# HGRN2 output products of a hybrid decoder layer: the eight products within the chunk first, then the eight with the state, all adding into one PSUM bank

## The chip, the cores and the metric

One core of one Trainium2 chip runs the whole program. The time is the device time of one execution in microseconds (us); less is better. TensorE (PE) multiplies, VectorE (DVE), ScalarE (ACT) and GpSimd (POOL) do the rest, SyncE (SP) issues the transfers.

## The reference, cut to what matters

One decoder layer: RMSNorm, a projection whose columns feed four mixers (S5, HGRN2, RWKV-7, pooling), an output projection, and a squared-ReLU MLP. There are 2048 prompt tokens, 32 sample tokens, width 1024, and four HGRN2 heads of 64. The change touches the HGRN2 mixer alone, which the reference computes chunk by chunk:

```python
o = jnp.einsum('bhts,bhsv->bhtv', att, vb) + jnp.einsum('bhtk,bhkv->bhtv', qb * jnp.exp(b), S)
b_last = b[:, :, -1:, :]
S = jnp.exp(b_last[:, :, 0, :])[..., None] * S + jnp.einsum('bhsk,bhsv->bhkv', kb * jnp.exp(b_last - b), vb)
```

The output `o` of a chunk is a sum of two products: the attention within the chunk with the values, and the scaled queries with the state `S` that the chunk before left. The state then moves on.

## The kernel before, in words

Tokens run in six blocks of 256 or 384 (the last also carries the 32 sample tokens). Each block goes through projection, mixers, output projection and MLP; the mixers of block b+1 are woven between the MLP products of block b. The large products (helper `mmg`, lines 157 to 159) take a split of both operands into a high and a low part, so that each weight tile gives three products of 128 rows by 128 columns of the array. Their weights arrive by DMA (`raw`), ScalarE makes the high part (`whi`, line 128), VectorE the low part (`wlo`, line 129). A scheduler at build time puts the recorded instructions of all lanes into one order for each engine, and each engine then works in that order, waiting on semaphores where it has to.

HGRN2 goes by pairs of chunks of 64 tokens (`hgrn_pair`): 2048 / 128 = 16 pairs, each with 4 heads h, of which head h lies in column j = h // 2 and on partitions 0 to 63 or 64 to 127 (hp = h % 2). At the end of a pair stand three sets of eight small fp32 products, which this text calls by their lines in the kernel before:

- line 1294, `pu`: what the pair adds to the state, `VK` (128 rows, 64 columns) with `VB`. Line 1297 on VectorE makes of it the state after chunk 0 and after chunk 1 of the pair (`S[1]` and `S[2]`; `S[0]` is left over from the pair before).
- line 1303, **inner products** in what follows: `VB` with the attention in `v`, into `po`. Each takes all 128 rows of the array and 64 of its columns, starting at column 0 for even heads and at column 64 for odd ones.
- line 1304, **state products**: `S[cp]` with the scaled queries `Q0`, added to the same place in `po`. Each takes 64 rows and 64 columns. With cp = 0 they need `S[0]`, with cp = 1 they need `S[1]`.

An fp32 product is two records in the trace, so eight products are 16 records, and the 16 pairs make 256 records of each line. `po` lies in one PSUM bank; `hgrn_out` then has ScalarE copy it (line 1407).

Of the kernel before, what the change touches and what calls it, by code (L numbers as in the profile page):

```python
# [606 lines left out]
class Mix(Main):  # L607
# [580 lines left out]
    def hgrn_pair(self, b, c0, pool):  # L1188
        nc = self.nc
        tt, ts, stt = nc.vector.tensor_tensor, nc.vector.tensor_scalar, nc.vector.scalar_tensor_tensor  # L1190
        act, mm = nc.scalar.activation, nc.tensor.matmul
# [5 lines left out]
        q, f, v, gt = P[:, 2:4, W], P[:, 4:6, W], P[:, 6:8, W], P[:, 8:10, W]  # L1197
# [17 lines left out]
        Q0 = T("lf")  # L1215
# [14 lines left out]
        VK, VB = T("VK", (128, 4, 64)), self.VB  # L1230
# [22 lines left out]
        for l0, l1 in ((-1, 2), (2, 6)):  # L1253
            pas = [self.px() for _ in range(2)]
            sec = {}
            for l in range(l0, l1):
                o0 = 0 if l < 0 else 64 * (l - l0) + (64 if l0 < 0 else 0)
                w = 64 if l < 0 else 32
                for hp in range(2):
# [3 lines left out]
                    for j in range(2):  # L1263
                        for cp in range(2):
                            o = 128 * j + 64 * cp
                            if l < 0:
                                a, c = k[hs, j, 64 * cp:64 * cp + 64], q[hs, j, 64 * cp:64 * cp + 64]
                            else:
                                h = LV[l]
# [6 lines left out]
            for l in range(l0, l1):  # L1276
                for hp in range(2):
                    o, d = v[:, :, 64 * hp:64 * hp + 64], sec[l, hp]
# [3 lines left out]
                    h = LV[l]  # L1282
# [6 lines left out]
        S = [self.S[:, (self.Si + i) % 3] for i in range(3)]  # L1289
        self.Si = (self.Si + 2) % 3  # L1290
        pu = self.px()[:, :256].rearrange("p (c j n) -> p c j n", c=2, j=2)
        for h in range(4):
            for cp in range(2):
                mm(pu[64 * (h % 2):64 * (h % 2) + 64, cp, h // 2, :], VK[:, h, :], VB[:, cp, h, :], start=True, stop=True)
        for cp in range(2):
            for j in range(2):
                stt(out=S[cp + 1][:, j, :], in0=S[cp][:, j, :], scalar=eb[:, j, 64 * cp + 63:64 * cp + 64], in1=pu[:, cp, j, :], op0=ALU.mult, op1=ALU.add)
        po = self.px()[:, :256].rearrange("p (j n) -> p j n", j=2)
        for h in range(4):
            o, j = slice(64 * (h % 2), 64 * (h % 2) + 64), h // 2  # L1300
            for cp in range(2):
                w = slice(64 * cp, 64 * cp + 64)
                mm(po[o, j, w], VB[:, cp, h, :], v[:, j, o], start=True, stop=False)  # L1303
                mm(po[o, j, w], S[cp][o, j, :], Q0[o, j, w], start=False, stop=True)  # L1304
        yield
        yield from self.hgrn_out(b, W, po, 256, T)

# [728 lines left out]
```

## Time and profile before

| | |
|---|---|
| median of three runs | 2759.57 us (2753.03 to 2764.25) |
| the profiled execution | 2760.78 us, span 2758.7 us |
| PE busy | 2676.0 us, 97% of the span |
| DVE, ACT, POOL busy | 71%, 52%, 13% |
| granted TensorE clock, mean | 0.982 |

The profile comes from one execution. Busy time of PE overlaps from product to product, since the end of a product in flight is modelled; how much room a product takes is better read from the distance between the starts of neighbours in the timeline.

### The profile page before, as it was taken

The page shows a single profiled execution, that of the slowest core. Times are in us where ns is not written, and L with a number is a line of the kernel's source. Part 1 is how long each engine was busy: PE and PEld are TensorE (multiplying, and loading weights), DVE is VectorE, ACT ScalarE, POOL GpSimd, SP SyncE. Part 2 cuts the span into 40 slices and gives each one's busy share as a digit, 9 for nine tenths or more (in the row PEclk, how much of TensorE's full clock was granted, in tenths as well). Part 3 has the DMA queues.
Part 4 walks back from the last instruction along what each step waited for, and adds up shares of the span by engine and source line. Part 5 has one row for each costly group of instructions (what it writes and reads, how often), then busy time and mean ns, then how long its engine had stood idle before and what let it go on. Part 6 is the DMA issues. An engine that isn't in the chain of part 4 may idle for free.

```text
span 2758.7 us, 52873 instructions
## 1 busy us (share of the span) xinstructions
PE 2676.0 (97%) x20466; PEld 2524.8 (92%) x20466; DVE 1960.4 (71%) x4324; ACT 1438.7 (52%) x2377; POOL 359.0 (13%) x864
## 2 busy tenths in 40 slices
PE   8799899999999999999999999999999999999998
PEld 8688799999999999999999999999999989989997
DVE  6885877875877777487777648776766776666666
ACT  6554756554655445365554536554454744445443
POOL 7631201101011100101110010111001101000000
PEclk9899999999999999999999999999999999999999
DMA  6543343464322355532225553223565223535443
GB/s 204 145 127 90 121 140 130 139 212 155 117 84 90 97 170 162 163 117 86 94 94 171 163 160 110 90 90 100 168 179 163 95 93 106 147 112 174 162 168 124
DMA packets 221068, 366.27 MB, mean 133 GB/s; under 512 B 105521, under 2 KB 140913, under 8 KB 220817
## 3 DMA queue, kind: packets, MB, share of 16 engines
q1 hardware_dynamic: 220816, 362.90, 42.1%
q8 instruction: 161, 2.64, 0.4%
q14 instruction: 91, 0.74, 0.1%
HBM read 343.26 MB, written 17.99 MB: 131 GB/s over the span
## 4 chain that ended last, share of the span: by engine, by line
PE 75%; DVE 8%; DMA 5%; ACT 3%; POOL 3%; issue 3%; SPq 2%; DVEq 0%; ACTq 0%; POOLq 0%
PE mm L157 21%; PE mm L158 21%; PE mm L159 20%; DMA raw<-w 2%; DVE wlo L129 2%; PE x L1272 1%; PE x L1304 1%; ACT whi L128 1%; PE x L1303 1%; POOL tm L885 1%; POOL XD L887 1%; PE x L687 1%; DMA xs<-xT 1%; DMA mt<-dB 1%; PE x L951 1%
## 5 line engine op out<-in xcount | busy, mean ns | idle before, releaser
L128 ACT CAST whi<-raw 128x1024 fp32r<-128x1024 f32 x552 | 577.5, 1046 | 785.5 <-PE mm L158 566.2
L157 PE MATMUL mm<-AB,whi 128*128 128x384 f32 (+2 forms) x2880 | 951.6, 331 | 14.5 <-ACT whi L128 6.1
L159 PE MATMUL mm<-AB,wlo 128*128 128x384 f32 (+2 forms) x2880 | 937.4, 326 | 5.9 <-DVE wlo L129 5.9
L158 PE MATMUL mm<-AB,whi 128*128 128x384 f32 (+2 forms) x2880 | 936.3, 326 | 0.8 <-DVE AB L199 0.6
L129 DVE TENSOR_TENSOR wlo<-raw,whi 128x1024 fp32r<-128x1024 f32 x552 | 678.8, 1230 | 269.6 <-ACT whi L128 267.0
L157 PEld LDWEIGHTS mm<-AB,whi 128*128 128x128 f32 x2880 | 547.9, 191 | 27.8 <-ACT whi L128 6.8
L159 PEld LDWEIGHTS mm<-AB,wlo 128*128 128x128 f32 x2880 | 548.7, 191 | 10.7 <-DVE wlo L129 8.0
L158 PEld LDWEIGHTS mm<-AB,whi 128*128 128x128 f32 x2880 | 548.9, 191 | 6.8 <-DVE AB L199 0.9
L157 PE MATMUL mm<-act,whi 128*128 128x384 f32 (+2 forms) x1536 | 497.0, 329 | 3.3 <-DVE h L338 2.1
L158 PE MATMUL mm<-act,whi 128*128 128x384 f32 (+2 forms) x1536 | 495.8, 324 | 0.5 <-DVE act L329 0.3
L159 PE MATMUL mm<-act,wlo 128*128 128x384 f32 (+2 forms) x1536 | 493.6, 323 | 0.0
L157 PEld LDWEIGHTS mm<-act,whi 128*128 128x128 f32 x1536 | 289.3, 190 | 10.9 <-DVE h L338 2.6
L158 PEld LDWEIGHTS mm<-act,whi 128*128 128x128 f32 x1536 | 291.4, 190 | 5.5 <-issue 1.8
L159 PEld LDWEIGHTS mm<-act,wlo 128*128 128x128 f32 x1536 | 291.1, 190 | 3.9 <-issue 2.4
L338 DVE TENSOR_TENSOR h<-h,mm 128x384 f32<-128x384 f32 (+2 forms) x384 | 192.9, 510 | 114.1 <-PE mm L159 113.3
L885 POOL TENSOR_TENSOR tm<-sq,XD 32x15 f32<-32x15 f32 (+7 forms) x240 | 97.9, 408 | 571.8 <-DMA sq<-XC 554.4
L329 DVE TENSOR_TENSOR act<-q,act 128x384 fp32r<-128x384 f32 (+2 forms) x192 | 99.6, 520 | 7.4 <-ACT q L326 3.3
L324 ACT ACTIVATE act<-r 128x384 fp32r<-128x384 f32 (+2 forms) x192 | 94.1, 490 | 14.2 <-DVE r L323 12.2
L880 POOL MEMSET XD<- 32x512 f32 x16 | 8.3, 516 | 604.6 <-PE x L969 570.1
L887 POOL TENSOR_TENSOR XD<-XD,tm 32x15 f32<-32x15 f32 (+7 forms) x240 | 80.2, 334 | 18.5
L192 DVE TENSOR_TENSOR acc<-acc,sq 128x384 f32<-128x384 f32 (+2 forms) x126 | 65.0, 516 | 12.7 <-ACT sq L191 10.0
L328 DVE TENSOR_TENSOR q<-r 128x384 f32<-128x384 f32 x128 | 71.9, 562 | 1.2 <-ACT r L321 1.0
(585 smaller groups left out, 3195.1 us busy)
## 6 DMA issues: line engine op xcount, KB each, us to landing
raw<-w SPq DMA_DIRECT2D x552, 512.0 KB
xs<-xT SPq DMA_DIRECT2D x96, 192.0 KB
yT<-xo SPq DMA_DIRECT2D x32, 192.0 KB
mt<-dB SPq DMA_DIRECT2D x20, 256.0 KB
mt<-dT SPq DMA_DIRECT2D x20, 256.0 KB
mt<-dC SPq DMA_DIRECT2D x20, 256.0 KB
xs<-xT SPq DMA_DIRECT2D x24, 144.0 KB
rt<-dRot SPq DMA_DIRECT2D x16, 98.0 KB
```

What stands on the lines that cost most here:

```text
L128: nc.scalar.copy(hi, raw)
L129: (nc.gpsimd if GW(i) else nc.vector).tensor_tensor(out=lo, in0=raw, in1=hi, op=ALU.subtract)
L157: nc.tensor.matmul(ps[:, :n], a, xh, start=k == ks[0], stop=False)
L158: nc.tensor.matmul(ps[:, :n], a, xl, start=False, stop=False)
L159: nc.tensor.matmul(ps[:, :n], c, xh, start=False, stop=k == ks[-1])
L192: nc.vector.tensor_tensor(out=acc[:, :n], in0=acc[:, :n], in1=q[:, :n], op=ALU.add)
L324: nc.scalar.activation(out=self.act[:, s, 0, :n], in_=r[:, :n], func=AF.Square)
L328: nc.vector.tensor_tensor(out=q[:, :n], in0=r[:, :n], in1=r[:, :n], op=ALU.mult)
L329: nc.vector.tensor_tensor(out=self.act[:, s, 1, :n], in0=q[:, :n], in1=self.act[:, s, 0, :n], op=ALU.subtract)
L338: nc.vector.tensor_tensor(out=self.h[:, d, :n], in0=self.h[:, d, :n], in1=ps[:, :n], op=ALU.add)
L885: g.tensor_tensor(out=w, in0=U[:, 0:t, t:t + 1].to_broadcast([32, t, m]), in1=XT[:, t:t + 1, t:16].to_broadcast([32, t, m]), op=ALU.mult)
L887: g.tensor_tensor(out=XT[:, 0:t, t:16], in0=XT[:, 0:t, t:16], in1=w, op=ALU.add)
```

## The change

The eight inner products of a pair are issued one after the other, then the eight state products. Both go through the same list of (j, cp, hp), in which hp changes fastest, and line 1294 goes through it too. Since all sixteen outputs now lie open in one bank at once, only the first product on each half of the partitions starts the bank afresh (`start`), and all others add or, where nothing was written since, overwrite. The number and sizes of products stay as they were.

```diff
+        jch = [(j, cp, hp, slice(64 * hp, 64 * hp + 64)) for j in range(2) for cp in range(2) for hp in range(2)]
-        for h in range(4):
-            for cp in range(2):
-                mm(pu[64 * (h % 2):64 * (h % 2) + 64, cp, h // 2, :], VK[:, h, :], VB[:, cp, h, :], start=True, stop=True)
+        for j, cp, hp, o in jch:
+            mm(pu[o, cp, j, :], VK[:, 2 * j + hp, :], VB[:, cp, 2 * j + hp, :], start=True, stop=True)
...
-        for h in range(4):
-            o, j = slice(64 * (h % 2), 64 * (h % 2) + 64), h // 2
-            for cp in range(2):
-                w = slice(64 * cp, 64 * cp + 64)
-                mm(po[o, j, w], VB[:, cp, h, :], v[:, j, o], start=True, stop=False)
-                mm(po[o, j, w], S[cp][o, j, :], Q0[o, j, w], start=False, stop=True)
+        for j, cp, hp, o in jch:
+            w = slice(64 * cp, 64 * cp + 64)
+            mm(po[o, j, w], VB[:, cp, 2 * j + hp, :], v[:, j, o], start=j == cp == 0, stop=False, skip_group_check=True)
+        for j, cp, hp, o in jch:
+            w = slice(64 * cp, 64 * cp + 64)
+            mm(po[o, j, w], S[cp][o, j, :], Q0[o, j, w], start=False, stop=j == cp == 1, skip_group_check=True)
```

In the new kernel the inner products are line 1302 and the state products line 1305; the scheduler orders the rest anew. On PE, a pair's small products stand in two clusters with large products between them. This is the first cluster of the seventh pair (the second pair of the third block; `AB` and `whi` belong to a large product), before:

```order
L159 MATMUL mm<-AB_78,wlo 128x384
L1294 MATMUL x<-VB,VK 64x64 x8
L1303 MATMUL x<-P_7462,VB 64x64
L1304 MATMUL x<-lf,S 64x64
L1303 MATMUL x<-P_7462,VB 64x64
L157 MATMUL mm<-AB_78,whi 128x384
```

and now:

```order
L159 MATMUL mm<-AB_78,wlo 128x384
L1294 MATMUL x<-VB,VK 64x64 x8
L1302 MATMUL x<-P_7462,VB 64x64 x8
L1305 MATMUL x<-lf,S 64x64 x2
L157 MATMUL mm<-AB_78,whi 128x384
```

The six inner products that were left over for later now stand here, and the two state products on `S[0]` of column 0 follow them. The second cluster of the same pair, before, with 21 large products between the two (the alternation goes on where the dots stand, to 13 products in all):

```order
L159 MATMUL mm<-AB_78,wlo 128x384
L1304 MATMUL x<-lf,S 64x64
L1303 MATMUL x<-P_7462,VB 64x64
L1304 MATMUL x<-lf,S 64x64
...
L157 MATMUL mm<-AB_78,whi 128x384
```

and now, with 18 large products between:

```order
L159 MATMUL mm<-AB_78,wlo 128x384
L1305 MATMUL x<-lf,S 64x64 x6
L157 MATMUL mm<-AB_78,whi 128x384
L158 MATMUL mm<-AB_78,whi 128x384
L159 MATMUL mm<-AB_78,wlo 128x384
```

The six state products that are left stand alone. Fourteen of the 16 pairs have no other product inside the run of eight inner products; in the fourth and the fifth pair the scheduler now puts some. This is the fourth pair (line 800 is a product of the RWKV-7 mixer with 64 rows), before:

```order
L1294 MATMUL x<-VB,VK 64x64 x8
L1303 MATMUL x<-P_1555,VB 64x64
L1304 MATMUL x<-lf,S 64x64
L1303 MATMUL x<-P_1555,VB 64x64
L800 MATMUL x<-P_2418,wl 128x128 x2
L157 MATMUL mm<-act,whi 128x256
```

and now:

```order
L1294 MATMUL x<-VB,VK 64x64 x8
L1302 MATMUL x<-P_1555,VB 64x64 x3
L800 MATMUL x<-P_2418,wl 128x128 x2
L1302 MATMUL x<-P_1555,VB 64x64 x5
L1305 MATMUL x<-lf,S 64x64 x2
L157 MATMUL mm<-act,whi 128x256
```

The second cluster of this pair follows after 8 large products, where it followed after 17.

## Rows read from the trace of the kernel before

**Rows 1.** The page's head, engines' busy time, and chain that ended last:

```profile
span 2758.7 us, 52873 instructions
PE 2676.0 (97%) x20466; PEld 2524.8 (92%) x20466; DVE 1960.4 (71%) x4324; ACT 1438.7 (52%) x2377; POOL 359.0 (13%) x864
PE 75%; DVE 8%; DMA 5%; ACT 3%; POOL 3%; issue 3%; SPq 2%; DVEq 0%; ACTq 0%; POOLq 0%
```

**Rows 2.** Busy time by stretch: length, each engine, PE clock, DMA share, GB/s:

```profile
150.00:640.00 490.00, 466.96 (x4285) 431.70 (x4285) 377.11 (x931) 280.06 (x483) 76.69 (x181) 0.97 0.44 137
640.00:1120.00 480.00, 478.08 (x3461) 452.69 (x3460) 339.00 (x735) 251.11 (x403) 48.01 (x115) 1.00 0.40 126
2080.00:2400.00 320.00, 312.66 (x2445) 294.33 (x2444) 220.28 (x540) 162.32 (x294) 34.60 (x77) 0.97 0.41 121
```

**Rows 3.** Groups from 640 to 2400 us: records | busy us, mean ns | idle before:

```profile
L1303 PE MATMUL x<-P,VB 128*64 128x64 f32 x176 | 28.6, 245 | 0.0
```

**Rows 4.** Chain that ended last, by line, from 640 to 2400 and from 150 to 640:

```profile
by line: PE mm L157 25.7%; PE mm L158 24.8%; PE mm L159 24.7%; PE x L1272 1.7%; PE x L1304 1.3%; PE x L1303 1.2%; PE x L687 1.1%; DMA raw<-w 1.0%; issue 0.9%; PE x L1827 0.7%; PE x L974 0.7%; PE x L1826 0.7%; PE x L969 0.7%; PE x L951 0.7%;
...
by line: PE mm L157 8.3%; PE mm L158 7.6%; PE mm L159 7.3%; issue 7.2%; DVE wlo L129 6.2%; DMA raw<-w 5.1%; ACT whi L128 3.8%; POOL tm L885 3.8%; POOL XD L887 3.5%; DMA xs<-xT 2.7%; PE x L1304 2.0%; PE x L1303 1.8%; DMA yT<-xo 1.4%; DMA XC<
```

**Rows 5.** Who waited for whom in the whole span: us, times, longest:

```profile
ACT whi L128 <- PE mm L158: 566.2, 244, 7.9
...
ACT whi L128 <- DMA raw<-w: 181.6, 101, 6.0
...
ACT eb L1407 <- PE x L1304: 42.7, 15, 8.1
```

**Rows 6.** PE timeline of the seventh pair: start us, length, line, rows*columns, records:

```profile
865.47 0.73 PE L1294 MATMUL x<-VB,VK 128*64 128x64 f32 x16
865.99 0.28 PE L1303 MATMUL x<-P,VB 128*64 128x64 f32 x2
866.20 0.33 PE L1304 MATMUL x<-lf,S 64*64 64x64 f32 x2
866.45 0.33 PE L1303 MATMUL x<-P,VB 128*64 128x64 f32 x2
866.71 0.45 PE L157 MATMUL mm<-AB,whi 128*128 128x384 f32 x1
867.00 0.34 PE L158 MATMUL mm<-AB,whi 128*128 128x384 f32 x1
867.17 0.34 PE L159 MATMUL mm<-AB,wlo 128*128 128x384 f32 x1
...
870.59 0.33 PE L1304 MATMUL x<-lf,S 64*64 64x64 f32 x2
870.85 0.33 PE L1303 MATMUL x<-P,VB 128*64 128x64 f32 x2
871.11 0.32 PE L1304 MATMUL x<-lf,S 64*64 64x64 f32 x2
...
873.67 0.33 PE L1304 MATMUL x<-lf,S 64*64 64x64 f32 x2
873.93 0.44 PE L157 MATMUL mm<-AB,whi 128*128 128x384 f32 x1
```

**Rows 7.** PE timeline near 983 us: state-sized products (line 964) without alternation:

```profile
983.58 0.68 PE L964 MATMUL x<-XD,Y 64*64 64x64 f32 x16
984.19 0.44 PE L158 MATMUL mm<-act,whi 128*128 128x384 f32 x1
```

**Rows 8.** PE timeline near 588 us: products that keep to one half of the columns:

```profile
588.42 0.68 PE L987 MATMUL x<-sv,M 128*64 128x64 f32 x8
589.03 0.44 PE L159 MATMUL mm<-AB,wlo 128*128 128x384 f32 x1
```

**Rows 9.** PE timeline near 1029 us: full-size pairs, line 1826 starts, line 1827 adds:

```profile
1029.31 0.39 PE L1826 MATMUL x<-U,mt 128*128 128x48 f32 x2
1029.53 0.39 PE L1827 MATMUL x<-S,mt 128*128 128x48 f32 x2
1029.75 0.39 PE L1826 MATMUL x<-U,mt 128*128 128x48 f32 x2
```

**Rows 10.** DVE timeline: line 1297 of the fourth and of the seventh pair:

```profile
445.03 0.47 DVE L1297 SCALAR_TENSOR_TENSOR S<-S,eb,x 128x64 f32<-128x64 f32 x2
...
870.14 0.47 DVE L1297 SCALAR_TENSOR_TENSOR S<-S,eb,x 128x64 f32<-128x64 f32 x2
...
872.00 0.27 DVE L1297 SCALAR_TENSOR_TENSOR S<-S,eb,x 128x64 f32<-128x64 f32 x1
```

**Rows 11.** PE timeline of the fourth pair: both clusters, in brackets idle before:

```profile
440.63 0.28 PE L1303 MATMUL x<-P,VB 128*64 128x64 f32 x2
...
445.36 0.33 PE L1304 MATMUL x<-lf,S 64*64 64x64 f32 x2 [1.07 <-DVE S L1297]
```

## The prediction

> **What bounds the kernel now.** I read the page first. The span is 2758.7 us, PE is busy in 97% of it, and the chain that ended last runs over PE for 75% [rows 1]. Then the busy time by stretch, to see whether this holds where the HGRN2 pairs stand: from 640 to 1120 us PE is busy for 478.08 of 480 us, and the two stretches of 480 us behind it read alike, while from 150 to 640 us it is busy for 466.96 of 490 [rows 2]. So from 640 us on PE has almost no idle time that could swallow a saving; before that 5% of the time is waits for others. Eleven of the 16 pairs lie after 640 us (176 of the 256 records of line 1303 [rows 3]), five before.
>
> Next I asked whether the products in question lie on the chain. From 640 to 2400 us lines 1304 and 1303 have 1.3% and 1.2% of it, 44 us of 1760 [rows 4]. Eleven pairs at 4.06 us each (worked out below) are 44.7 us: all of that time is on the chain. From 150 to 640 us it is 2.0% and 1.8%, 18.6 us of 490 [rows 4], and four pairs and a second cluster lie there: again nearly all of it.
>
> Last, whether the weights could keep up with a faster PE. ScalarE waited 566.2 us in 244 places for PE to give back a buffer before it could make the next `whi`, and 181.6 us for the transfer of the raw weights [rows 5]. The supply is held back by PE more often than by its transfers, so it has room.
>
> **What the alternation costs.** The timeline of the seventh pair shows the price. The eight products of line 1294, all of one shape and one behind the other, take from 865.47 to 865.99: 0.52 us, 0.065 each. Then the alternation begins. From 865.99 to 866.71 there are three products (0.72 us), and from 870.59 to 873.93 thirteen (3.34 us): 4.06 us for sixteen, 0.25 each [rows 6]. Over 16 pairs this is 65 us. Two differences could be the reason: inner products take 128 rows of the array and state products 64, so each follows one of another shape; or each state product adds to what the product just before it wrote. The pairs of lines 1826 and 1827, where each second product adds to the first one's place, answer this: 0.22 us from 1826 to 1827 and 0.22 us back, with no extra time for adding, and both take the full array [rows 9]. Eight products of line 964, which have the shape of state products and do not alternate, take 0.61 us from 983.58 up to the large product behind them, exit included [rows 7]. So the change of shape is what costs.
>
> **The change part by part.** The first cluster becomes eight inner products behind line 1294, of its shape, then two state products. Seven inner products at 0.065 make 0.455; the eighth, with the change of shape behind it, is 0.21 (865.99 to 866.20); the first state product is 0.065, and the second, with the exit to a large product, 0.26 (866.45 to 866.71 has such an exit) [rows 6]. That is 0.99 us in place of 0.72: 0.27 more. The second cluster becomes six state products. Line 964's eight with exit are 0.61 [rows 7]; two fewer at 0.06 leave 0.49, in place of 3.34: 2.85 less. Entry from the large products is there before and after. A pair gains 2.58 us, and 16 pairs gain 41.
>
> Bounds of this: eight records, that is four products, of line 987, which stay in one half of the columns, take 0.61 us up to the large product [rows 8]. Less an exit of 0.26 that is 0.117 for each product but the last. If products cost as much even in runs, the first cluster is 7 x 0.117 + 0.21 + 0.117 + 0.26 = 1.41 and the second 0.61 + 2 x 0.117 = 0.84, the pair gains 1.81, and all 29 us. I take the price of lines 1294 and 964 instead, since the new list changes halves with every product, as line 964 does and as line 1294 does with every second one. At 0.05 each, a little under any row shown, the gain would be 43 us. At 0.25, unchanged, it is nothing (a rival below).
>
> The Trainium skill, TensorE: Matmul & The Clock Gate, has in its section on packing small matmuls that a weight load overlaps products in flight only if its rows of the array differ; in the section on LDWEIGHTS it gives P / 1.2 ns for P columns. Inner products all take the same 128 rows, so two loads of 64 columns would cost 107 ns each time, and the gain would be some 5 us less by an estimate from that page. The row of line 1294 speaks against it, with 65 ns for a product whose rows are always the same [rows 6].
>
> Line 1294 in the new order: its halves alternate at every product in place of every second. I cost this at nothing; the most it can give is the difference of 0.065 to 0.05 for 128 products, 2 us.
>
> Two things are taken back. In the fourth and fifth pair another lane's products split the run of inner products; each split adds two changes of shape of 0.25 - 0.065 = 0.19 us, together under 1 us. And the second cluster now comes sooner, but needs the state that line 1297 on VectorE makes. In the seventh pair line 1297's two instructions run from 870.14 to 870.61, the first done by about 870.41 (0.27 for one), and the cluster begins at 870.59 [rows 6, 10]. Now it would come 0.27 later for the first cluster and three large products sooner (about 0.175 each, as 867.00 to 867.17 [rows 6]): at 870.33, so it waits about 0.1 us. In the fourth pair PE waited for it already, 1.07 us up to 445.36, since line 1297 began at 445.03 [rows 10, 11]. Nine large products fewer stand before it now, at about 0.12 each for 256 columns, against 0.27 for the first cluster and 0.38 for the split: about 0.45 us more of waiting. Behind the waiting product on PE stand the other state products and then the large ones; nobody on VectorE waits for them. In all I take 1 us for waits, 1 for splits.
>
> VectorE's instructions keep their order around line 1297 except for a few places, and ScalarE's copy of `po`, which waited 42.7 us for line 1304 in 15 places [rows 5], gets it sooner by the time that the cluster shrinks; ScalarE is busy 52% of the span [rows 1], so that I count nothing for it.
>
> Where the stretch up to 640 us is bound by others, a saving on PE is partly given back to waits. Five pairs at 2.58 are 12.9 us; I take a third of it off, 4 us, a choice between nothing (the chain has it all) and all of it.
>
> **Sum.** 41 - 1 - 1 - 4 = 35 us. The profiled execution took 2760.78 us, so 2726; it lies 1.2 us above the median of the runs, and against that the time is 2759.57 - 35, about 2725.
>
> **The rivals.**
> - *Row halves of one bank get in each other's way.* The state products of even and odd heads take different rows of the array and write the same bank one right behind the other. If each had to wait for the other to leave, they would stay at 0.25 us. A first cluster of 7 x 0.065 + 0.21 + 0.25 + 0.26 = 1.18 and a second of 6 x 0.25 = 1.5 make 2.68, a gain of 1.38 a pair, 22 in all, 16 after the same deductions: 2744. Line 964 speaks against it, in which halves of the rows share a bank too, at 0.61 us for eight [rows 7]. The Trainium skill, TensorEngine Tiling (Array Packing), Gotcha 1, says that different row tiles cannot access the same PSUM bank simultaneously; by that rule this rival would hold, and the trace does not bear it out. Chance 5%.
> - *The saving is lost to the supply of weights.* PE needs its weights 35 us sooner over the span; ScalarE's 181.6 us of waits for raw weights show that transfers are late at times [rows 5]. If half the saving becomes waits for weights, the time is 2760 - 17, about 2743. Against it: 566.2 us in which the supply waited for PE. Chance 8%.
> - *The alternation isn't the cost.* If the price of 0.25 belongs to these operands or to adding into `po`, nothing is gained: about 2760. Lines 1826 and 1827 speak against it [rows 9]. Chance 4%.
> - *Slower: PE waits for the state.* All six state products of the second cluster stand behind one that needs line 1297. If the state came later than the cluster by more than the 2.58 us that a pair gains, the pair would lose. At 4 us in every pair this is 16 x 1.4 = 23 us more, 2783. In the latest pair shown the state was 1.07 us late [rows 11], in the seventh 0.18 us early [rows 6, 10]. Chance 2%.
>
> **How the numbers follow.** The forecast, a gain of 21 to 46 us, has 81%; its own range is 2714 to 2739. The upper end of 46 is 43 for cheaper products, 2 for line 1294, and no deductions, with 1 for what a new order may give; the lower end of 21 is the price of line 987 less deductions, with 2 for a new order. To hold 8 in 10 with the cases of half a gain I go up to 2743 and leave out the rest. A measurement of this kernel can tell some 0.5%, 14 us, from no change. Faster than that: the forecast and most of the first two rivals, 0.91. Within it: 0.07. Slower: 0.02.
>
> **What would show it.** Right: lines 1302 and 1305 each in runs with starts some 0.06 us apart per product, the second cluster about 0.5 us long up to the large product behind it, the first about 1.0; the busy time of the two lines, now 65 us by starts, some 24; PE's share of the span unchanged. PE's idle time in front of line 1305 should stay under 3 us. Wrong: records of line 1305 still 0.1 to 0.15 us apart (halves of a bank), or clusters short but more idle time of PE in front of line 157 with `whi` or `wlo` named (supply), or long waits for line 1297.

## The result, and the profile after

The changed kernel takes 2719.98 us (median of 4 runs, 2714.48 to 2722.89), the kernel before beside it 2760.21 (4 runs, 2753.03 to 2764.25): ratio 0.9855, with an interval from 0.9829 to 0.9881. That is 40 us less, or 1.45%. A later set of runs, told below, gave 0.9854 (0.9836 to 0.9871).

The page of the changed kernel (its profiled execution took 2714.48 us), to be read beside [rows 1]; the last line is the chain that ended last, by engine:

```profile
span 2712.6 us, 52883 instructions
...
PE 2629.4 (97%) x20466; PEld 2492.0 (92%) x20466; DVE 1955.7 (72%) x4324; ACT 1438.6 (53%) x2377; POOL 357.5 (13%) x864
...
PE 74%; DVE 11%; DMA 5%; ACT 4%; POOL 3%; issue 2%; SPq 1%; DVEq 0%; ACTq 0%; POOLq 0%
```

PE has the same 20466 records, is busy 46.6 us less than the 2676.0 of before, and the span is shorter by 46.1: between these two executions the whole saving is busy time of PE. Its share of the span stays at 97%, so PE is still the bound.

Where the time went is seen in the timeline of PE in the seventh pair, beside [rows 6] (inner products are now line 1302, state products line 1305):

```profile
857.06 0.69 PE L1294 MATMUL x<-VB,VK 128*64 128x64 f32 x16
857.58 0.64 PE L1302 MATMUL x<-P,VB 128*64 128x64 f32 x16
858.14 0.33 PE L1305 MATMUL x<-lf,S 64*64 64x64 f32 x4
858.41 0.44 PE L157 MATMUL mm<-AB,whi 128*128 128x384 f32 x1
...
861.78 0.56 PE L1305 MATMUL x<-lf,S 64*64 64x64 f32 x12
862.27 0.44 PE L157 MATMUL mm<-AB,whi 128*128 128x384 f32 x1
```

The eight inner products, 16 records, are now one row, since nothing stands between them. Start to start, the first cluster is 858.41 - 857.58 = 0.83 us (it has ten products now; the three of before took 0.72) and the second 862.27 - 861.78 = 0.49 (3.34 before). A pair costs 1.32 us in place of 4.06. It gains 2.74, and 16 pairs like it 43.8 us. Line 1294 takes 0.52 us (857.06 to 857.58), as before.

The waits that the prediction named, in the whole span (us, times, longest), beside [rows 5]; the last line is from the list of PE's own waits:

```profile
ACT whi L128 <- PE mm L158: 528.0, 232, 6.8
...
ACT whi L128 <- DMA raw<-w: 203.0, 111, 6.2
...
ACT eb L1408 <- PE x L1305: 9.2, 3, 4.6
...
PE x L1305 <- DVE S L1297: 1.8, 1, 1.8
```

PE waits for the state once, 1.8 us. ScalarE's copy of `po` waits 9.2 us in place of 42.7, as the products before it end sooner. ScalarE's waits for raw weights grew from 181.6 to 203.0 us, and those for PE shrank from 566.2 to 528.0, so the supply is nearer to PE than before, but it still waits for PE more than twice as long as for its transfers.

**Where the gain is kept, and where it is given back.** Line 1294 opens each pair, so its starts mark how far the program has come. This table sets its starts in the first execution of each kernel beside those in a second one (two of the experiments below, in which each kernel was run again):

| us | before | after | gain | before, again | after, again | gain |
|---|---|---|---|---|---|---|
| fifth pair starts | 514.11 | 501.33 | 12.8 | 515.43 | 502.00 | 13.4 |
| sixth pair starts | 786.92 | 782.27 | 4.7 | 789.00 | 783.30 | 5.7 |
| sixteenth pair starts | 2305.73 | 2262.04 | 43.7 | 2298.01 | 2265.21 | 32.8 |
| span ends | 2758.7 | 2712.6 | 46.1 | 2753.1 | 2717.1 | 36.0 |

In both columns of gain some 8 us are lost between the fifth and the sixth pair, although the fifth pair itself gains about 2.5 (its run of inner products is split): some 10 us are given back in one place. The busy time by engine over exactly this stretch, of before and then of after (PE, PEld, DVE, ACT, POOL, then granted clock, DMA share, GB/s):

```profile
514.11:786.92 272.81, 268.14 (x1972) 255.72 (x1971) 201.27 (x431) 150.51 (x251) 35.24 (x79) 0.99 0.48 151
...
540.00:580.00 40.00, 36.61 (x365) 34.37 (x364) 33.72 (x74) 17.07 (x28) 0.64 (x2) 0.96 0.64 195
```

```profile
501.33:782.27 280.94, 271.44 (x1971) 259.28 (x1970) 200.72 (x429) 152.38 (x251) 34.98 (x79) 0.98 0.47 145
...
535.10:541.00 5.90, 5.79 (x26) 5.64 (x27) 4.86 (x9) 2.04 (x3) 0.00 (x0) 0.50 0.60 193
605.90:612.60 6.70, 6.70 (x25) 6.70 (x25) 3.26 (x7) 3.04 (x5) 0.00 (x0) 0.50 0.49 161
```

The work is the same, but PE's idle time grew from 272.81 - 268.14 = 4.67 us to 9.50, and its busy time by 3.3 although the fifth pair took about 2.5 off it, so by some 5.8. The last two lines show where most of that comes from: for 5.9 and 6.7 us the granted clock was 0.50, the lower level of 1.2 GHz. Before was not free of this: 0.96 over the 40 us from 540 to 580 is 3.2 us at half the clock. Ahead of both stretches of the new kernel, PE had stood idle for some 2.5 us, as its timeline shows (in brackets the idle time and what ended it):

```profile
535.16 0.58 PE L157 MATMUL mm<-act,whi 128*128 128x256 f32 x1 [2.52 <-ACT whi L128]
...
604.05 0.42 PE L1827 MATMUL x<-U,mt 128*128 128x48 f32 x2 [2.40 <-DMA mt<-dT]
```

So two longer waits, one for converted weights and one for a transfer, and 12.6 us at half the clock behind them in place of 3.2, swallow a quarter of the gain. The first experiment shows that PE's being early is not needed for such a loss.

### The profile page after: what moved, and what is told of

It is laid out like the page before. It is cut to its first block, busy times and chain, and to the rows that moved or that the text cites. A ratio compares the mean times of both kernels' runs of the same rounds, so it can differ in the third digit from the quotient of the medians.

```text
span 2712.6 us, 52883 instructions
## 1 busy us (share of the span) xinstructions
PE 2629.4 (97%) x20466; PEld 2492.0 (92%) x20466; DVE 1955.7 (72%) x4324; ACT 1438.6 (53%) x2377; POOL 357.5 (13%) x864
## 4 chain that ended last, share of the span: by engine, by line
PE 74%; DVE 11%; DMA 5%; ACT 4%; POOL 3%; issue 2%; SPq 1%; DVEq 0%; ACTq 0%; POOLq 0%
PE mm L157 21%; PE mm L158 21%; PE mm L159 21%; DVE wlo L129 3%; DMA raw<-w 2%; PE x L1272 1%; ACT whi L128 1%; POOL XD L887 1%; POOL tm L885 1%; DMA xs<-xT 1%; PE x L687 1%; PE x L1828 1%; PE x L1827 1%; DMA mt<-dB 1%; PE x L951 1%
## 5 line engine op out<-in xcount | busy, mean ns | idle before, releaser
L128 ACT CAST whi<-raw 128x1024 fp32r<-128x1024 f32 x552 | 577.5, 1046 | 773.0 <-PE mm L158 528.0
L885 POOL TENSOR_TENSOR tm<-sq,XD 32x15 f32<-32x15 f32 (+7 forms) x240 | 90.7, 378 | 563.0 <-DMA sq<-XC 545.6
```

Source lines behind the costliest of these rows:

```text
L128: nc.scalar.copy(hi, raw)
L885: g.tensor_tensor(out=w, in0=U[:, 0:t, t:t + 1].to_broadcast([32, t, m]), in1=XT[:, t:t + 1, t:16].to_broadcast([32, t, m]), op=ALU.mult)
```

## The experiments

Where an experiment's diff has only the products, the rest of the kernel is that of the new one unless the text says otherwise.

**All of the change but the grouping.** The new order of line 1294, the new order over heads and chunks, and the flags (one start for the bank, one stop) are kept; each inner product is followed by its state product again.

```diff
         for j, cp, hp, o in jch:
             w = slice(64 * cp, 64 * cp + 64)
             mm(po[o, j, w], VB[:, cp, 2 * j + hp, :], v[:, j, o], start=j == cp == 0, stop=False, skip_group_check=True)
-        for j, cp, hp, o in jch:
-            w = slice(64 * cp, 64 * cp + 64)
             mm(po[o, j, w], S[cp][o, j, :], Q0[o, j, w], start=False, stop=j == cp == 1, skip_group_check=True)
```

> Line 1294 in the new order, the new list of (j, cp, hp), the new start flags, but each inner product is again followed by its state product. Theory (the change of shape costs): 4.06 us a pair as before, time 2760, within 0.3% of the kernel before. Rival (the new flags or the order of the halves give the gain): about 2720.

2762.57 us against 2757.32 for before beside it: ratio 1.0016 (0.9997 to 1.0035), no difference clear of the noise. Its PE timeline has 11 products in its second cluster of the seventh pair:

```profile
877.27 0.32 PE L1303 MATMUL x<-lf,S 64*64 64x64 f32 x2
877.53 0.33 PE L1302 MATMUL x<-P,VB 128*64 128x64 f32 x2
...
879.84 0.33 PE L1303 MATMUL x<-lf,S 64*64 64x64 f32 x2
880.09 0.44 PE L159 MATMUL mm<-AB,wlo 128*128 128x384 f32 x1
```

880.09 - 877.27 = 2.82 us, 0.256 a product. Flags and orders give nothing without the grouping. It also bears on the 10 us given back: from its fifth to its sixth pair this kernel, whose PE is hardly early (the fifth pair starts at 513.08), takes 281.69 us too, with 274.73 of PE's busy time and clusters as long as before's:

```profile
513.08:794.77 281.69, 274.73 (x1971) 261.80 (x1970) 200.09 (x429) 152.19 (x251) 35.66 (x79) 0.97 0.47 144
```

**The alternation kept, in one shape.** Before's order and flags; the state product reads all 128 rows of the state, and its other operand has zeros in the rows of the other head, so that it computes the same with the shape of an inner product. The zeros and products are made by POOL and VectorE ahead of it.

```diff
...
+                for hp in range(2):
+                    nc.gpsimd.memset(Qz[64 - 64 * hp:128 - 64 * hp, hp], 0.0)
+                    tt(out=Qz[64 * hp:64 * hp + 64, hp], in0=q[64 * hp:64 * hp + 64], in1=eb[64 * hp:64 * hp + 64], op=ALU.mult)
...
-                mm(po[o, j, w], S[cp][o, j, :], Q0[o, j, w], start=False, stop=True)
+                mm(po[o, j, w], S[cp][:, j, :], Qz[:, h % 2, j, w], start=False, stop=True)
```

> The old alternation and flags, but state products made 128 rows by 64 columns, the shape of the inner products: the scaled queries lie in two buffers in which the other half of the partitions is zero (two GpSimd memsets and one more VectorE product a pair). Theory (shape): neighbours 0.06 to 0.07 us apart although they alternate and add to the place just written; 13 products in about 1.0 us in place of 3.34; time 2720 to 2730. Rival (adding to the place just written costs): 0.25 apart still, 2760 or more.

2729.62 us: ratio 0.9896 (0.9859 to 0.9932), 28 us less, though every state product still follows the inner product to which it adds. Its PE timeline (line 1306 inner, 1307 state):

```profile
866.12 0.28 PE L1306 MATMUL x<-P,VB 128*64 128x64 f32 x2
866.24 0.28 PE L1307 MATMUL x<-QK,S 128*64 128x64 f32 x2
866.36 0.28 PE L1306 MATMUL x<-P,VB 128*64 128x64 f32 x2
...
870.79 0.27 PE L1307 MATMUL x<-QK,S 128*64 128x64 f32 x1 [0.26 <-DVE S L1300]
...
871.77 0.28 PE L1307 MATMUL x<-QK,S 128*64 128x64 f32 x2
871.99 0.44 PE L157 MATMUL mm<-AB,whi 128*128 128x384 f32 x1
```

Neighbours stand 0.12 us apart in one half of the columns, not the 0.06 to 0.07 expected, and thirteen products take 1.20 us (870.79 to 871.99), not about 1.0, where before took 3.34. With the order unchanged and the shape made one, most of the price is gone. By its clusters, 0.45 (866.12 to 866.57) and 1.20, a pair gains 2.41 and 16 pairs 38.6 us; the time moved by 28. Of what the first five pairs gain nothing is left where the sixth starts: 790.75, against 786.92 and 789.00 in the two executions of before.

**Two shapes, two places.** Before's alternation, but the state products write the other half of the bank (`pi`), with a start of their own; ScalarE copies them out and VectorE adds the two. This takes the adding to one place away and leaves the shapes.

```diff
-                mm(po[o, j, w], VB[:, cp, h, :], v[:, j, o], start=True, stop=False)
-                mm(po[o, j, w], S[cp][o, j, :], Q0[o, j, w], start=False, stop=True)
+                mm(po[o, j, w], VB[:, cp, h, :], v[:, j, o], start=True, stop=True)
+                mm(pi[o, j, w], S[cp][o, j, :], Q0[o, j, w], start=True, stop=True)
...
```

> The old alternation with its two shapes, but state products start afresh in the other half of the bank, and ScalarE and VectorE add the two halves (one more instruction each a pair). Theory (shape): still 0.25 us a product, 2760 to 2768. Rival (adding to the place just written costs): 0.06 to 0.07 us apart, about 2720.

2774.67 us, above the expected 2760 to 2768: ratio 1.0065 (1.0042 to 1.0087). Its thirteen products take 889.33 - 886.00 = 3.33 us, the 3.34 of before:

```profile
886.00 0.33 PE L1305 MATMUL x<-lf,S 64*64 64x64 f32 x2
886.25 0.33 PE L1304 MATMUL x<-P,VB 128*64 128x64 f32 x2
...
889.08 0.33 PE L1305 MATMUL x<-lf,S 64*64 64x64 f32 x2
889.33 0.44 PE L157 MATMUL mm<-AB,whi 128*128 128x384 f32 x1
```

So adding into one place costs nothing. The 17 us more come with the copy and the addition in 16 pairs. In its trace this kernel is 7.8 us behind the first execution of before where the fifth pair starts (521.94), 14.8 where the sixth does (801.71), and 15.2 at the end (span 2773.9): what it loses, it loses before the sixth pair. What holds PE up there was not followed further.

**Half the grouping.** For each head its two inner products, then its two state products: the shape changes 7 times inside a pair in place of 15.

```diff
-        for j, cp, hp, o in jch:
...
+        for j, hp in [(j, hp) for j in range(2) for hp in range(2)]:
+            o = slice(64 * hp, 64 * hp + 64)
+            for cp in range(2):
+                mm(po[o, j, 64 * cp:64 * cp + 64], VB[:, cp, 2 * j + hp, :], v[:, j, o], start=j == cp == 0, stop=False, skip_group_check=True)
+            for cp in range(2):
+                mm(po[o, j, 64 * cp:64 * cp + 64], S[cp][o, j, :], Q0[o, j, 64 * cp:64 * cp + 64], start=False, stop=j == cp == 1, skip_group_check=True)
```

> The new kernel with groups of two: for each head two inner products, then two state products; 7 changes of shape a pair in place of 1 in the new kernel and 15 in the kernel before. Theory: each change costs 0.19 us more than a product without one, so 6 x 0.19 x 16 = 18 us more than the new kernel, about 2738. A rival in which only groups of eight help: 2760.

2734.86 us: ratio 0.992 (0.9888 to 0.9952), 22 us less, between before and the full grouping. Its PE timeline:

```profile
863.94 0.33 PE L1305 MATMUL x<-lf,S 64*64 64x64 f32 x2
864.19 0.45 PE L1303 MATMUL x<-P,VB 128*64 128x64 f32 x4
864.57 0.44 PE L1305 MATMUL x<-lf,S 64*64 64x64 f32 x4
...
866.43 0.44 PE L157 MATMUL mm<-AB,whi 128*128 128x384 f32 x1
```

A group of two products takes 0.37 to 0.38 us: 0.25 for the one with the change of shape behind it, 0.12 for the one that stays (both of a group lie in one half of the columns). Each change counts, wherever it stands. The time came near the expected 2738 by two misses, though. The clusters, 0.59 (859.46 to 860.05) and 2.49, make 3.08 us a pair, 28 over 16 pairs more than the new kernel's rather than 18, since products that stay cost 0.12 rather than 0.06; and this kernel does not give the 10 us back between the fifth and the sixth pair (272.05 us).

**The new kernel again**, beside the next two, to measure more finely.

> The new kernel once more, unchanged, for a second trace and as the yardstick of the two kernels beside it: 2715 to 2723. If the clusters give 2.73 us a pair, they do so again at all 16 pairs; if the stretches at half clock behind the second clusters of the kernel before went away with the alternation, there are none behind the clusters here either. Rival: their absence in the first trace was chance, and some come back.

2718.49 us against 2758.58: ratio 0.9854 (0.9836 to 0.9871), with the same clusters (the second again 0.49). From the sixth pair on the clock did not fall behind any of them, but it fell twice elsewhere (last section).

**State products with the later ones first.** The state products that need line 1297 come first, so that all eight stand in the second cluster and the first has one shape only.

```diff
...
-        for j, cp, hp, o in jch:
+        for cp, j, hp in [(cp, j, hp) for cp in (1, 0) for j in range(2) for hp in range(2)]:
...
```

> The new kernel with the state products that need the new state first in the list, so that the scheduler puts all eight into the second cluster of 15 pairs: one change of shape fewer in the first cluster. Theory: 0.19 us a pair less, 3 us in all, about 2717; the wait for the state in front of the second cluster, 4.0 us in the new kernel's trace, stays. Rival: more work behind the wait makes it longer, 2720 to 2730.

2715.42 us (2711.50 to 2725.78): ratio 0.9855 (0.9835 to 0.9874), not to be told from the new kernel's. Its timeline:

```profile
858.76 0.64 PE L1302 MATMUL x<-P,VB 128*64 128x64 f32 x16
859.33 0.44 PE L157 MATMUL mm<-AB,whi 128*128 128x384 f32 x1
...
862.87 0.68 PE L1305 MATMUL x<-lf,S 64*64 64x64 f32 x16
863.48 0.45 PE L158 MATMUL mm<-AB,whi 128*128 128x384 f32 x1
```

0.57 and 0.61 us make 1.18 a pair in place of 1.32: 2.2 us over 16 pairs, less than the runs differ among themselves. PE waited for line 1297 2.0 us in 2 places, against 1.8 in one; the 4.0 that the expectation names has waits of the weight loads in it.

**Halves of the array in long runs.** The list of products has the half of the columns in its outermost loop, so that four products in a row keep one half (for state products, of the rows too). Shapes are grouped as in the new kernel.

```diff
-        jch = [(j, cp, hp, slice(64 * hp, 64 * hp + 64)) for j in range(2) for cp in range(2) for hp in range(2)]
+        jch = [(j, cp, hp, slice(64 * hp, 64 * hp + 64)) for hp in range(2) for j in range(2) for cp in range(2)]
```

> The new kernel with the half of the partitions (even and odd heads) changing slowest in the list, so that four products in a row keep to one half of the columns. No change of shape is added. By the price of line 987 (0.117 us a product in one half) inner and state products and line 1294 cost some 0.9 us more a pair, 14 us in all, about 2734. Rival: the halves do not matter, 2720.

2729.05 us: ratio 0.9897 (0.988 to 0.9913), 10.6 us above the new kernel beside it (2718.49). Its timeline:

```profile
860.13 0.79 PE L1294 MATMUL x<-VB,VK 128*64 128x64 f32 x13
...
861.60 0.32 PE L1305 MATMUL x<-lf,S 64*64 64x64 f32 x2
861.86 0.45 PE L157 MATMUL mm<-AB,whi 128*128 128x384 f32 x1
...
865.22 0.84 PE L1305 MATMUL x<-lf,S 64*64 64x64 f32 x14
865.99 0.45 PE L157 MATMUL mm<-AB,whi 128*128 128x384 f32 x1
```

From line 1294 on, its two clusters take 1.73 + 0.77 = 2.50 us, those of the new kernel 1.35 + 0.49 = 1.84 (858.41 - 857.06, and the second). That is 0.66 a pair and 10.6 us over 16: what the medians differ by (the spans of the two traced executions differ by 5.0). Changing halves is worth a quarter of what grouping the shapes is.

**The kernel before again**, one look.

> The kernel before, unchanged, for a second trace. From line 1294 of the fifth pair to that of the sixth it took 272.8 us in the first trace, and the new kernel 281.0 and 281.3 in its two. If the new kernel gives time back there, because it comes sooner to transfers that have not landed, this trace shows 273 again; if the stretch varies from one execution to the next, it may show about 280, and the give-back falls. If the alternation is what makes the clock fall to half behind the second clusters of the sixth, ninth, twelfth and fifteenth pair, it falls again at some of them.

2754.84 us. From the fifth to the sixth pair it took 273.57 us, as the first execution did. Its ten intervals from the sixth to the sixteenth pair, beside those of the first execution of before and of the two of the new kernel, in this order:

```profile
789.00:2298.01 1509.01, 1500.96 (x11114) 1417.72 (x11113) 1069.04 (x2357) 792.54 (x1303) 157.83 (x384) 1.00 0.40 125
```

```profile
786.92:2305.73 1518.81, 1508.67 (x11114) 1424.85 (x11113) 1069.88 (x2357) 792.14 (x1303) 158.06 (x384) 0.99 0.40 125
```

```profile
782.27:2262.04 1479.77, 1470.38 (x11114) 1395.60 (x11113) 1067.57 (x2357) 792.22 (x1303) 156.81 (x384) 1.00 0.41 128
```

```profile
783.30:2265.21 1481.91, 1473.37 (x11114) 1398.45 (x11113) 1067.55 (x2357) 792.77 (x1303) 155.38 (x384) 1.00 0.41 128
```

The same 11114 records on PE each time. The second execution of before and of the new kernel differ by 1500.96 - 1473.37 = 27.6 us of busy time, and ten pairs at 2.74 make 27.4: the clusters account for it. The first execution of before has 7.7 us of busy time more than the second. Its clock fell at the end of the second clusters of the sixth, ninth, twelfth and fifteenth pair (behind all but the last stand eight products of line 964), as these windows of it show:

```profile
796.00:800.50 4.50, 4.50 (x31) 4.18 (x32) 0.85 (x2) 1.19 (x3) 0.00 (x0) 0.62 0.40 117
1277.50:1281.50 4.00, 4.00 (x27) 3.88 (x27) 0.85 (x2) 1.19 (x3) 0.00 (x0) 0.57 0.34 135
1758.50:1762.70 4.20, 4.20 (x28) 4.13 (x26) 0.84 (x2) 1.19 (x3) 0.00 (x0) 0.59 0.28 111
2236.50:2244.50 8.00, 8.00 (x40) 6.97 (x40) 5.04 (x9) 2.14 (x4) 0.00 (x0) 0.57 0.19 66
```

In such a stretch large products of 384 columns stand 0.32 us apart (1759.39 to 1759.71) in place of 0.175. By the windows' clock the four stretches at the lower level make some 17 us together; by an estimate from the two spacings they lose 17 x (1 - 0.175 / 0.32) = 7.7 us: the difference.

That the clock falls again behind some of these clusters did not come true: in this second execution it was 1.00 behind all four (799.00 to 802.50, 1277.00 to 1280.50, 1754.00 to 1759.00 and 2233.00 to 2240.00).

## Why the prediction was right, point by point

- **What bounds the kernel, and what the alternation costs.** Right, and shown. PE's busy time and the span shrank by the same 46 us in the first executions; in the second ones busy time shrank by 47.5 (2676.7 to 2629.2), idle time grew by 11.4, and 36.0 were left. Of the two reasons weighed, the change of shape is the cause: with one shape a product of the alternation takes at most 0.12 us (alternation in one shape), without adding to one place it still takes 0.256 (two places), flags and order alone give nothing (all but the grouping), and with 7 changes in place of 15 the clusters give 0.98 of the 2.74 us a pair (half the grouping). The Trainium skill, TensorEngine Tiling (Array Packing), Key Properties, says that changing the tiling mode drains TensorE. The runs agree as far as they go, with 0.25 against 0.06 us a product; a drain as such is in no row.
- **The size of the clusters.** The second was 0.49, as worked out. The first was 0.83 in place of 0.99: eight inner products with the change of shape took 0.56 (857.58 to 858.14) and the two state products with the exit 0.27, where 0.67 and 0.33 were expected. The seven inner products cost 0.05 each, the price that the prediction gave as a bound and called a little under any row shown; line 964's row has it already, (0.61 - 0.26) / 7. A pair gained 2.74 rather than 2.58, all 43.8 rather than 41. Line 1294 gained nothing, as taken.
- **What is taken back.** This is the term that was mis-sized. Waits for the state: 1.8 us in place of 1. The early stretch: 4 us were taken off, as a third of what five pairs gain; of the 13.7 that five pairs gain by their clusters, 4.7 and 5.7 were left where the sixth pair starts, so that 8 to 9 went. Nor was it spread over the stretch: the first four pairs kept more than their clusters give (12.8 and 13.4 against 11.0), and some 10 us went between the fifth and the sixth pair. The second executions add up: 5.7 at the sixth pair, 27.1 over the next ten (27.4 by the clusters) and 3.2 from the sixteenth on make the 36.0 by which their spans differ. The medians differ by 40, which would fit executions of before in which the clock falls, 7.7 us longer in the one shown. The time of before does go with its clock: of 15 runs of it, that with the highest mean clock, 0.986, took 2746.31 us and that with the lowest, 0.976, 2770.48. But the eight runs of the new kernel have 0.979 to 0.984, inside that range, so that the clock makes these 4 us is not shown. The prediction had no such term: that 35 came within 5 us of the result owes something to luck, to two sizes, too small each, with opposite signs.
- **Why the stretch after the fifth pair is longer is not settled.** Two waits and the half clock behind them are shown. Neither PE's coming early nor the grouping is needed for it: the kernel with all but the grouping is hardly early and takes 281.69 us there, and the one with two places, whose fifth pair starts 7.8 us later than before's, takes 279.77. Of the ten executions traced, seven take 279.23 to 281.69 at a mean clock of 0.97 or 0.98, and three take 272.05 to 273.57 at 0.99: both of before, and half the grouping. What tells the two kinds apart was not tried.
- **Row halves of one bank** fell: state products of alternating row halves stand 0.06 us apart in line 1305. The Trainium skill, TensorEngine Tiling (Array Packing), Gotcha 1, says that different row tiles cannot access the same PSUM bank simultaneously. No wait for that shows here (0.06 us), where the two row halves write different partitions of one bank; whether both are in it at one instant is in no row.
- **The weight-load rule** of TensorE: Matmul & The Clock Gate in the Trainium skill, with its estimate of 5 us less gain, is not borne out as far as the halves of the columns alternate (0.06 to 0.07 us a product). Where neighbours of one shape keep one half, they stand 0.12 us apart (alternation in one shape, half the grouping), near the 107 ns that are estimated from that page for two loads; that the loads are what takes this time is in no row. The lower bound of the prediction would have been about right for another order (halves of the array in long runs: 29.5 us less than before).
- **Supply of weights**: PE waited 6.1 us in front of line 157 for `whi` and 5.9 in front of line 159 for `wlo` before, 7.7 and 3.8 after, so 12.0 against 11.5: no part of the saving went there in all, though the waits for `whi` are longer. **PE waits for the state**: 1.8 us in one place. **The alternation isn't the cost**: fell with the runs.

## What to carry to other kernels

Count the changes of the array's shape in the order of small products: here each cost 0.19 us, three times the product itself, and ordering by shape was worth 40 us of 2760 without taking one product away. Within a shape let neighbours take different halves of the columns; four in a row in one half cost 10.6 us here. Where flags, operands and order change at once, one kernel that keeps the order and makes the shapes equal, and one that keeps the shapes and changes the place, tell which of them paid.

## What the runs showed of the hardware that was not expected

- The clock can fall behind PE work that has no idle time in it: in one execution of before it was 0.5 for some 17 us in all at the end of four of the alternating clusters of 3.3 us, and in the kernel with two places, which alternates too, behind the clusters of the sixth and the ninth pair (0.57 from 811.50 to 815.50, 0.50 from 1293.00 to 1296.40). In the other execution of before it was 1.00 there, and in the kernel with all but the grouping too, so the alternation does not decide it alone, and what does stays open. Behind the new kernel's short clusters from the sixth pair on it did not fall in either execution. But in the second one it was 0.50 from 1926.80 to 1930.20, behind 3.2 us of small products of lines 974, 1827 and 1828, with PE busy for 11.57 of the 11.80 us ahead and no HGRN2 product near, and once more from 2176.00 to 2179.40.
- Two waits of 2.5 us on a busy PE can cost more than their 5 us: 12.6 us at half the clock follow them, 9.4 more than before had there. By an estimate from the spacing of large products these lose 9.4 x (1 - 0.175 / 0.32) = 4.3 us more, most of the 5.8 by which busy time grew.
